# FFN's first products in another order, operands' sums product by product, and the final norm's last squares summed by TensorE

## The chip, the cores and the metric

The kernel runs on one core of one Trainium2 chip. The metric is the device time of one execution in microseconds (us), the median over several runs. Line numbers are those of the kernel before; the profile gives one execution, instruction by instruction.

## The reference

One layer on a sequence of 1024 rows with 1024 channels, float32. What matters here comes after the two mixers:

```python
mix = jnp.einsum('bsd,de->bse', g_a * y_a + g_b * y_b, w_o[l])
x = x + g1 * mix
h2 = rms_norm(x, norm_ffn_g[l]) * (1.0 + sc2) + sh2
a, bgate = jnp.split(jnp.einsum('bsd,df->bsf', h2, w_ffn_in[l]), 2, axis=-1)     # 1024 -> 2 x 2816
x = x + g2 * jnp.einsum('bsf,fd->bsd', jax.nn.silu(a) * bgate, w_ffn_out[l])
return rms_norm(x, final_norm_g)
```

## The kernel before, in words

**Layout and precision.** Activations lie with channels on the 128 partitions and the sequence along the free axis, in two halves of 512 columns (KC = 8 blocks of 128 channels, KH = 4 is half of them). Each float32 operand is split in a high part, rounded by ScalarE (`wh`, `t2h` and so on, a cast), and a low part, the difference, made by VectorE (`wl`, `t2l`). A product of two such operands is three matmuls (`mm3`, lines 289, 290 and 292: high by high, high by low, low by high).

**Duals.** The FFN's input matrix is worked off in N_IN = 11 duals. A dual is two column blocks of weights by two halves of the sequence, computed with seven products in place of eight, in the order `PRODUCTS = "1265734"`. Each product is 24 matmuls of 128x512: two banks p of 4 blocks k of 3. Operands of the products: 1 and 2 take parts of h2 as they are (`h20` to `h27`, the first half of the sequence); 6 takes `t2`; 5 takes `t1`; 7 takes `t3`; 3 takes `b22`; 4 takes `t4`. These are sums and differences of h2's quarters; they are the same for every dual and are made once, at the start of the FFN. Products 1, 6, 7 and 4 accumulate one after the other in the banks x, products 5 and 3 in the banks z, product 2 in y; ahead of each next product that accumulates there, the bank must have been read (`in_evac`: copies by ScalarE for 1, 6 and 5, additions by VectorE for 2, 7 and 3).

**Weights.** `load` issues a 512 KB DMA on SP's queue into one of five buffers `raw` (`raw_tile`); a later load waits until a buffer is free. `split_w` casts (line 208) and subtracts (line 209). `next_w` keeps two units of the list `plan` ahead of the product that runs. In `dual_units` the blocks 11 and 12 are the weights of products 1 and 2; 6, 5, 7 and 3 need sums of blocks (lines 231, 232, 233 and 235). A dual with `early` loads its blocks one by one as units need them, and block 11 twice; otherwise product 1's unit loads all four.

**The start of the FFN.** The order before is: products 1 and 2 of dual 0, then of dual 1; then dual 0's other five; then dual 1's; then duals 2 to 10, seven each. While the first four run, the second half's norm is finished: `mix` evicts the output projection (line 813) and sums the squares (line 821), an `ss` matmul adds over partitions (line 410), and `rstd_end` (lines 344 to 346) makes two Newton-type steps on ScalarE's approximate reciprocal root. `norm_2_half(k)` then makes one fourth of t2; `norm_2_last` makes all operands for products 5, 7, 3 and 4. `tc.issue_after(ins)` puts what it encloses behind `ins` in its engine's list; apart from such rules the order on each engine comes from the framework's scheduler.

**The end.** The output product's last part runs in `PIECES` of 512, 256 and 256 columns. `piece_out` does one block j of 8: 12 matmuls, an eviction on VectorE (line 1078), a square on ScalarE (line 1081) and, for blocks scaled on GpSimd, a multiplication by the final gain (line 1085). `piece_sum` adds the squares on VectorE (line 1090). The norm of a piece is begun after block NORM_AT = 2 of the next one and its scaling after block NORM_AT + 3; the last piece's follow its last block. `piece_scale` multiplies by the reciprocal root: pieces 0 and 1 on GpSimd, in the last piece blocks 0, 3 and 5 on GpSimd (line 1101) and five on VectorE (line 1103), and issues the output DMAs.

Of the kernel before, what the change touches and what calls it, by code (L numbers as in the profile page):

```python
# [39 lines left out]
P = 128  # L40
D = 1024
T = 1024
# [48 lines left out]
NORM_AT = 2  # L91
LAG = 2
POOL_LAST = (0, 3, 5)
# [13 lines left out]
FILL = 272  # L107
# [3 lines left out]
def block_kernel(ctx: ExitStack, tc: tile.TileContext, x0, xT, c, vecs, ada, w_first, w_plain, w_duals,  # L111
# [102 lines left out]
    def dual_units(mats, n, early=False, eng=nc.vector):  # L214
# [7 lines left out]
        def unit(m):  # L222
            if early:
                get(*{"1": ("11",), "2": ("12",), "6": ("21", "22", "11"), "3": ("12",), "4": ("22",)}.get(m, ()))
            elif m == "1":
                get("11", "12", "21", "22")
            if m in "12":
                return split_w(a["1" + m], n, (), eng)
            if m == "6":
                a["s1"] = a["22"] if early else raw_tile(n)  # L230
# [70 lines left out]
    def product(banks, m, t, evac=None, between=None, y_tile=ps2_tile):  # L301
# [4 lines left out]
        for p in range(2):  # L306
            if m in "125":
                banks[b, p] = (y_tile if b == "y" else ps_tile)(b)
# [18 lines left out]
    def t_split(src, hi, lo):  # L327
        nc.scalar.copy(hi, src)  # L328
        t_split.ins = nc.vector.tensor_tensor(lo, src, f32(hi), ALU.subtract).ins  # L329
# [528 lines left out]
    def norm_2_last():  # L858


        def splits(m, name, srcs):
            for k, src in enumerate(srcs):
                ts[m][k] = t_pair(name)
                t_split(src, *ts[m][k])
# [3 lines left out]
        with tc.issue_after(t_split.ins):  # L868
            splits("5", "t1", [x1[k][:, halves[0]] for k in range(KH)])
            for k in range(KH):  # L870
                nc.vector.tensor_tensor(b12[k], b22[k], b12[k], ALU.subtract)
        with tc.issue_after(t_split.ins):
            splits("7", "t3", b12)
        with tc.issue_after(t_split.ins):
            splits("3", "b22", b22)
        with tc.issue_after(t_split.ins):
            for k in range(KH):
                minus(b21[k], t2[k], b21[k])
            splits("4", "t4", b21)
# [12 lines left out]
    in_units = [dual_units([w_fi[d, m] for m in range(4)], 1024, d < 2) for d in range(N_IN)]  # L892
    in_order = [(d, m) for d in range(2) for m in "12"] + [(d, m) for d in range(2) for m in PRODUCTS[2:]]
    in_order += [(d, m) for d in range(2, N_IN) for m in PRODUCTS]

    def in_unit(d, m):
        if (d, m) == (1, "6"):
            with tc.issue_after(t_split.ins):
# [12 lines left out]

    def in_evac(d):
        def evac(p, m, ps):
# [6 lines left out]
            elif m == "7":  # L920
                t = ha[f, "5"]
                nc.vector.tensor_tensor(t, ps, t, ALU.add)
                nc.scalar.activation(t, t, AF.Silu, scale=-1.0)
            elif m == "3":
                t = ha[f, "6"]
                nc.vector.tensor_tensor(t, ps, t, ALU.add)
# [49 lines left out]
    def in_product(d, m):  # L976
        product(in_banks[d], m, ts[m], in_evac(d), y_tile=ps_tile if d == 1 else ps2_tile)
        if d == N_IN - 1:
            group_load(0, m)

    def norm_2_start():
        nonlocal r2
        r2 = norm_start(sums[1], "r2")

    r2 = None
    product(in_banks[0], "1", ts["1"], in_evac(0), norm_2_start)
    r2 = rstd_end(*r2)
    for i, (d, m) in enumerate(in_order[1:4]):
        norm_2_half(i, r2)
        in_product(d, m)  # L990
    norm_2_half(KH - 1, r2)
    norm_2_last()
    close(*phase_1)
    raws.append(open_pool("raw_a", 1, side="right", stack=ctx)[1])
    x1ap = open_pool("x1a", 2, side="right", stack=ctx)[1]
    phase_2 = [open_pool("gi", 7), open_pool("stage", 3, side="right")]
    gip, stagep = (p for _, p in phase_2)
    for d, m in in_order[4:]:
# [4 lines left out]
        if m == PRODUCTS[-1]:  # L1003
            if 2 <= d < 6:
                with tc.issue_after(in_evac.ins):
                    for i in range(40 + 2 * (d - 2), 42 + 2 * (d - 2)):
                        modulation(i, x1ap.tile([P, T], F32, tag="x1", name="ada"))
# [61 lines left out]
    def piece_out(i, j):  # L1069
# [14 lines left out]
        if on_pool(i, j):  # L1084
            nc.scalar.activation(dst, dst, AF.Copy, scale=col(V_GFIN, j))
# [113 lines left out]
```

## Time and profile before

| what | value |
|---|---|
| median of 3 runs | 1516.14 us (1514.99 to 1517.78) |
| the profiled execution's own time | 1518.37 us |
| its span in the profile | 1516.6 us |
| mean granted TensorE clock | 0.992 |
| busy: TensorE, VectorE, ScalarE, GpSimd | 1480.1, 1177.6, 612.7, 582.0 us |
| the FFN's first product starts | near 853.7 us |
| the last matmul of the output product | 1501.54 us |

Times in the views count from the span's start. PE is TensorE, DVE VectorE, ACT ScalarE, POOL GpSimd, SP the queue that issues loads. A row of a timeline holds start, duration, engine, line, operation, output<-inputs, and in brackets the idle time before it with its releaser. A row of the waits holds who waited for whom, the total in us, the number of times and the longest. "x2" merges two instructions.

### The profile page before, as it was taken

How to read it: one execution, taken by the hardware profiler on the slowest of the kernel's cores; microseconds unless marked ns; L12 is line 12 of the kernel's file. 1: busy time of each engine (PE TensorE's matmuls, PEld its weight loads, DVE VectorE, ACT ScalarE, POOL GpSimd, SP SyncE). 2: the span in 40 equal slices, each digit the busy share in tenths (PEclk: the TensorE clock that was granted, in tenths of full speed). 3: DMA queues.
4: the chain of work that ended last, by engine and by line, in shares of the span. 5: the costliest groups of instructions: out<-in, count | busy, mean ns of one | idle time of the engine just before them, and what ended most of it. 6: DMA issues, size and time to landing. Idle time of an engine off the chain costs nothing.

```text
span 1516.6 us, 17958 instructions
## 1 busy us (share of the span) xinstructions
PE 1480.1 (98%) x6529; PEld 1211.6 (80%) x6529; DVE 1177.6 (78%) x1566; ACT 612.7 (40%) x871; POOL 582.0 (38%) x483
## 2 busy tenths in 40 slices
PE   9999999999998999999999989999999999999996
PEld 5788887877886888888788868888888888888886
DVE  7897898999998881858877798777777665676756
ACT  4654333433332442335335464444444443212234
POOL 0037788788768884320121001000111016535005
PEclk9999999999999999999999999999999999999998
DMA  9512223223222159647765436455554449999303
GB/s 345 207 63 84 84 70 139 70 97 111 98 83 87 66 198 393 242 152 223 251 207 163 143 97 193 156 179 179 181 172 158 155 152 365 354 292 282 124 15 112
DMA packets 87307, 255.66 MB, mean 169 GB/s; under 512 B 10033, under 2 KB 12209, under 8 KB 87218
## 3 DMA queue, kind: packets, MB, share of 16 engines
q1 hardware_dynamic: 46384, 146.30, 28.9%
q0 software_dynamic: 36944, 95.44, 19.1%
q10 hardware_dynamic: 3890, 12.78, 2.1%
q8 instruction: 51, 0.84, 0.2%
q14 instruction: 38, 0.31, 0.1%
HBM read 187.89 MB, written 66.58 MB: 168 GB/s over the span
## 4 chain that ended last, share of the span: by engine, by line
PE 50%; DVE 1%; ACT 1%; issue 0%; DVEq 0%; ACTq 0%
PE x L289 7%; PE x L290 7%; PE x L292 7%; PE z L289 4%; PE z L290 4%; PE z L292 4%; PE y L290 3%; PE y L289 3%; PE y L292 3%; PE mix L289 2%; PE mix L290 2%; PE mix L292 2%; PE yb L289 1%; PE yb L290 1%; PE yb L292 1%
## 5 line engine op out<-in xcount | busy, mean ns | idle before, releaser
L208 ACT CAST wh<-raw 128x1024 fp32r<-128x1024 f32 (+2 forms) x257 | 259.1, 1009 | 422.9 <-PE x L290 107.3
L209 POOL TENSOR_TENSOR wl<-raw,wh 128x1024 fp32r<-128x1024 f32 x92 | 238.0, 2594 | 86.5 <-ACT wh L208 80.1
L209 DVE TENSOR_TENSOR wl<-raw,wh 128x1024 fp32r<-128x1024 f32 (+2 forms) x165 | 188.2, 1141 | 52.4 <-ACT wh L208 50.2
L663 DVE SCALAR_TENSOR_TENSOR c<-diff,vec,c 128x512 f32<-128x512 f32 x248 | 182.3, 749 | 6.4 <-DMA q<-qs 2.6
L942 POOL DMA_DIRECT2D hid<-stage x71 | 37.9, 534 | 356.5 <-DVE stage L329 351.0
L289 PE MATMUL x<-th,wh 128*128 128x512 f32 x336 | 130.8, 389 | 0.0
L292 PE MATMUL x<-th,wl 128*128 128x512 f32 x336 | 130.7, 389 | 0.0
L290 PE MATMUL x<-tl,wh 128*128 128x512 f32 x336 | 130.7, 389 | 0.0
L663 DVE SCALAR_TENSOR_TENSOR c<-u,wsum,c 128x512 f32<-128x512 f32 x112 | 84.0, 750 | 7.1 <-issue 5.1
L292 PE MATMUL x<-t2h,wl 128*128 128x512 f32 x184 | 72.9, 396 | 4.2 <-POOL wl L209 4.2
L289 PE MATMUL x<-t2h,wh 128*128 128x512 f32 x184 | 72.2, 394 | 2.8 <-ACT t2h L328 2.4
L289 PEld LDWEIGHTS x<-th,wh 128*128 128x128 f32 x336 | 63.1, 188 | 13.3 <-issue 0.2
L290 PEld LDWEIGHTS x<-tl,wh 128*128 128x128 f32 x336 | 63.1, 188 | 13.1
L292 PEld LDWEIGHTS x<-th,wl 128*128 128x128 f32 x336 | 63.1, 188 | 13.1
L290 PE MATMUL x<-t2l,wh 128*128 128x512 f32 x184 | 72.5, 394 | 0.0
L231 POOL TENSOR_TENSOR raw<-raw 128x1024 f32<-128x1024 f32 x12 | 29.3, 2439 | 99.5 <-DVE wl L209 95.7
L292 PE MATMUL z<-th,wl 128*128 128x512 f32 x168 | 65.5, 390 | 0.0
L289 PE MATMUL z<-th,wh 128*128 128x512 f32 x168 | 65.4, 389 | 0.0
L290 PE MATMUL z<-tl,wh 128*128 128x512 f32 x168 | 65.4, 389 | 0.0
L328 ACT CAST stage<-g 128x512 fp32r<-128x512 f32 x62 | 38.3, 621 | 56.4 <-DMA hid<-stage 33.4
L270 DVE CUSTOM_DVE_ANT_0 raw<-raw,cs,vec 128x1024 f32<-128x1024 f32 x24 | 34.1, 1424 | 32.3 <-DMA raw<-in_ada 20.0
L329 DVE TENSOR_TENSOR stage<-g,stage 128x512 fp32r<-128x512 f32 x62 | 42.3, 687 | 21.7 <-ACT stage L328 21.6
(799 smaller groups left out, 4095.3 us busy)
## 6 DMA issues: line engine op xcount, KB each, us to landing
hid<-stage POOLq DMA_DIRECT2D x71, 512.0 KB, 4.8
raw<-in_w_fi SPq DMA_DIRECT2D x50, 512.0 KB, 4.2
raw<-in_w_duals SPq DMA_DIRECT2D x48, 512.0 KB, 3.5
th<-hid POOLq DMA_DIRECT2D x71, 256.0 KB, 6.1
tl<-hid POOLq DMA_DIRECT2D x71, 256.0 KB, 6.2
ada<-in_ada SPq DMA_DIRECT2D x24, 512.0 KB, 6.0
raw<-in_ada SPq DMA_DIRECT2D x24, 512.0 KB, 4.7
raw<-in_w_fo SPq DMA_DIRECT2D x24, 384.0 KB, 6.0
```

The source lines that it names most:

```text
L208: nc.scalar.copy(wh, raw)
L209: lo = lo_engine.tensor_tensor(wl, raw, f32(wh), ALU.subtract)
L231: eng.tensor_tensor(a["s1"], a["21"], a["22"], ALU.add)
L270: nc.vector.tensor_tensor_reduce(out=raw, in0=raw, in1=cs, scale=1.0, scalar=col(V_ADA, b), op0=ALU.mult, op1=ALU.add, accum_out=modc(b),)
L289: nc.tensor.matmul(ps, wh, xh, start=first, stop=False, skip_group_check=again)
L290: nc.tensor.matmul(ps, wh, xl, start=False, stop=False, skip_group_check=again)
L292: mm3.ins = nc.tensor.matmul(ps, wl, xh, start=False, stop=last, skip_group_check=again).ins
L328: nc.scalar.copy(hi, src)
L329: t_split.ins = nc.vector.tensor_tensor(lo, src, f32(hi), ALU.subtract).ins
L663: tap.ins = nc.vector.scalar_tensor_tensor(out=out, in0=src[:, s : s + H], scalar=wt, in1=acc, op0=ALU.mult, op1=ALU.add).ins
L942: nc.gpsimd.dma_start(hid_dram[key], s)
```

## The change

Five things are changed together.

- **Order.** Dual 2's product 1 runs after dual 1's product 2, ahead of dual 0's product 6. Dual 2's blocks are loaded in two steps (11 alone for product 1; 12, 21, 22 and 11 again for product 2), and its banks x are copied only ahead of its product 2. The banks y of dual 1 and z of duals 0 and 2 come from the pool of two banks (`ps2`).
- **Sums product by product.** `norm_2_last` is replaced by `norm_2_sums(m)`, called for m = 5, 7, 3 and 4 ahead of dual 0's product m; each is put behind the splits of the one before on VectorE and ScalarE. So are the weight units of dual 0's products 7, 3 and 4, and dual 0's additions to the banks of 7 and 3 (`behind_sums`, VectorE alone).
- **Final norm's steps.** The Newton step is written in two VectorE instructions with a square on ScalarE (`piece_norm`, `piece_rstd`); the sign that this changes is taken back by a negated gain `ngf`. The intermediate lies in PSUM, in the last piece the result too, with a copy in SBUF for GpSimd (`rp`).
- **Last squares.** In the last piece the squares of the last three blocks are not added by VectorE; `ss` is summed by TensorE from four operands.
- **Places.** NORM_AT is 1 instead of 2, the scaling follows two blocks later instead of three, and an unused fill tile has 264 columns instead of 272.

The diff, cut to its core:

```diff
-NORM_AT = 2
+NORM_AT = 1
 LAG = 2
+APART = 3
...
-FILL = 272
+FILL = 264
...
         def unit(m):
-            if early:
+            if early == 2:
                 get(*{"1": ("11",), "2": ("12",), "6": ("21", "22", "11"), "3": ("12",), "4": ("22",)}.get(m, ()))
+            elif early:
+                get(*{"1": ("11",), "2": ("12", "21", "22", "11")}.get(m, ()))
...
     def t_split(src, hi, lo):
-        nc.scalar.copy(hi, src)
+        t_split.act = nc.scalar.copy(hi, src).ins
...
-    def norm_2_last():
...
-        with tc.issue_after(t_split.ins):
-            splits("5", "t1", [x1[k][:, halves[0]] for k in range(KH)])
+    def norm_2_sums(m):
...
+        with tc.issue_after(t_split.ins), tc.issue_after(t_split.act):
             for k in range(KH):
-                nc.vector.tensor_tensor(b12[k], b22[k], b12[k], ALU.subtract)
...
+                if m == "7":
+                    nc.vector.tensor_tensor(b12[k], b22[k], b12[k], ALU.subtract)
+                elif m == "4":
+                    minus(b21[k], t2[k], b21[k])
             for k in range(KH):
-                minus(b21[k], t2[k], b21[k])
-            splits("4", "t4", b21)
+                ts[m][k] = t_pair("t" + m)
+                t_split({"5": x1[k][:, halves[0]], "7": b12[k], "3": b22[k], "4": b21[k]}[m], *ts[m][k])
...
-    in_units = [dual_units([w_fi[d, m] for m in range(4)], 1024, d < 2) for d in range(N_IN)]
-    in_order = [(d, m) for d in range(2) for m in "12"] + [(d, m) for d in range(2) for m in PRODUCTS[2:]]
-    in_order += [(d, m) for d in range(2, N_IN) for m in PRODUCTS]
+    EARLY = [2, 2, 1] + [0] * (N_IN - 3)
+    in_units = [dual_units([w_fi[d, m] for m in range(4)], 1024, EARLY[d]) for d in range(N_IN)]
+    in_order = [(0, "1"), (0, "2"), (1, "1"), (1, "2"), (2, "1")] + [(d, m) for d in range(2) for m in PRODUCTS[2:]]
+    in_order += [(d, m) for d in range(2, N_IN) for m in PRODUCTS if (d, m) != (2, "1")]
...
     def in_unit(d, m):
-        if (d, m) == (1, "6"):
-            with tc.issue_after(t_split.ins):
+        if (d, m) in ((0, "7"), (0, "3"), (0, "4"), (1, "6")):
+            with tc.issue_after(t_split.ins), tc.issue_after(t_split.act):
...
-    def in_product(d, m):
-        product(in_banks[d], m, ts[m], in_evac(d), y_tile=ps_tile if d == 1 else ps2_tile)
+    def in_product(d, m, between=None):
+        late = EARLY[d] == 1
+        if late and m == "2":
+            for p in range(2):
+                in_evac(d)(p, "1", in_banks[d]["x", p])
+        product(in_banks[d], m, ts[m], None if late and m == "1" else in_evac(d), between,
+                z_tile=ps2_tile if d in (0, 2) else ps_tile)
...
-    norm_2_half(KH - 1, r2)
-    norm_2_last()
...
+    for i, (d, m) in enumerate(in_order[5:]):
+        if i < 4:
+            norm_2_sums("5734"[i])
...
     def piece_scale(i, rf):
         at, n = PIECES[i]
         m = H // n
+        if i == LAST:
+            rp = wide_tile("rp")[:, :n]
+            nc.scalar.copy(rp, rf)
+        else:
+            rp = rf
...
-                    nc.gpsimd.tensor_tensor(y, src, rf, ALU.mult)
+                    nc.gpsimd.tensor_tensor(y, src, rp, ALU.mult)
...
-    def piece_norm(i, acc):
-        return norm_start(acc, "rf", PIECES[i][1], wide_tile)
+    def piece_norm(i, parts):
+
+        n = PIECES[i][1]
+        ss, r, q = (t[:, :n] for t in (ps_tile("ss"), wide_tile("rf"), wide_tile("rq")))
+        for part in parts:
+            nc.tensor.matmul(ss, ones, part, start=part is parts[0], stop=part is parts[-1])
+        rstd_start(ss, eps1, "rf", n, lambda name: r)
+        nc.scalar.activation(q, r, AF.Square, scale=0.5 ** 0.5)
+        return ss, r, q
+
+    def piece_rstd(i, ss, r, q):
+
+        n = PIECES[i][1]
+        t = ps2_tile("rft")[:, :n]
+        nc.vector.scalar_tensor_tensor(out=t, in0=ss, scalar=EPS, in1=q, op0=ALU.add, op1=ALU.mult)
+        out = ps2_tile("rf")[:, :n] if i == LAST else r
+        nc.vector.scalar_tensor_tensor(out=out, in0=t, scalar=1.5, in1=r, op0=ALU.subtract, op1=ALU.mult)
+        return out
...
-            if j > lag:
+            if j > lag and j - lag < KC - APART * (i == LAST):
                 piece_sum(i, j - lag)
...
-                norm = piece_norm(i - 1, acc)
-            if i and j == NORM_AT + 3:
+                norm = piece_norm(i - 1, [acc])
+            if i and j == NORM_AT + 2:
...
-        for j in range(KC - lag, KC):
-            piece_sum(i, j)
-    piece_scale(LAST, rstd_end(*piece_norm(LAST, sqs[0])))
+    piece_scale(LAST, piece_rstd(LAST, *piece_norm(LAST, [sqs[0]] + sqs[KC - APART :])))
```

58 lines of the change are left out of this document (28 added, 30 removed).

## The prediction

> **What bounds the kernel now.** I read the page's busy table first, then TensorE's waits over the whole run.
>
> ```profile
> span 1516.6 us, 17958 instructions
> PE 1480.1 (98%) x6529; PEld 1211.6 (80%) x6529; DVE 1177.6 (78%) x1566; ACT 612.7 (40%) x871; POOL 582.0 (38%) x483
> ...
> PE ss L410 <- DVE sq L1090: 3.9, 1, 3.9
> PE z L289 <- ACT g L917: 3.7, 1, 3.7
> PE x L289 <- ACT t2h L328: 2.4, 1, 2.4
> ...
> PE lead L289 <- ACT h11h L364: 1.4, 1, 1.4
> ```
>
> TensorE is busy 98% of the span, so only its holes can be won. The change touches the three rows that open the wait list: two where the FFN's first products begin (z, x) and one in the last norm (ss). After the last matmul nothing hides VectorE, so there every instruction on the path counts.
>
> The first place by the table of windows (us; then TensorE, its weight loads, VectorE, ScalarE, GpSimd busy; granted clock; DMA):
>
> ```profile
> 870.91:876.35 5.44, 5.44 (x25) 4.50 (x24) 5.44 (x9) 3.27 (x5) 0.00 (x0) 1.00 0.33 96
> 876.35:908.78 32.43, 26.30 (x97) 19.82 (x96) 29.05 (x43) 19.90 (x31) 0.00 (x0) 0.89 0.31 98
> 884.73:888.14 3.41, 3.41 (x9) 2.65 (x8) 3.41 (x7) 3.26 (x6) 0.00 (x0) 0.50 0.00 0
> 901.79:905.20 3.41, 3.41 (x9) 2.64 (x10) 3.38 (x6) 2.77 (x4) 0.00 (x0) 0.50 0.86 303
> 860.79:907.68 46.89, 40.76 (x162) 31.78 (x161) 43.46 (x64) 27.83 (x44) 0.00 (x0) 0.93 0.29 90
> ```
>
> Row one is an undisturbed product, dual 1's product 2: 24 matmuls in 5.44 us. Row two is dual 0's products 6, 5, 7 and 3: 96 matmuls, 21.8 us at that pace, which took 32.43. So 10.7 us are lost: 6.1 idle (2.4 and 3.7), 3.4 in the two half-clock stretches of rows three and four (1.7 each), 1.2 in small waits. The last row is VectorE from the second norm's first Newton step to the end of dual 1's sums: 43.5 of 46.9 us busy. VectorE feeds all of this, so any work put on it there comes out later.
>
> **Part 1: dual 2's product 1 goes ahead of dual 0's product 6.** It adds 5.44 us of matmuls as cover, and takes them out of the steady part later, where TensorE is the bound. It also adds one 512 KB load (dual 2's 11 block comes twice), and all later loads move back one place in SP's queue. That queue is paced by VectorE, since a load starts when a weight split has freed its buffer:
>
> ```profile
> 848.69 1.22 DVE L231 TENSOR_TENSOR raw<-raw 128x1024 f32<-128x1024 f32 x1 [3.13 <-DMA raw<-in_w_fi]
> 850.50 1.21 DVE L209 TENSOR_TENSOR wl<-raw,wh 128x1024 fp32r<-128x1024 f32 x1
> 853.75 0.75 DVE L813 SCALAR_TENSOR_TENSOR x<-mix,mod,xr 128x512 f32<-128x512 f32 x1 [1.44 <-PE mix L292]
> 854.65 1.23 DVE L209 TENSOR_TENSOR wl<-raw,wh 128x1024 fp32r<-128x1024 f32 x1
> 860.79 0.69 DVE L344 SCALAR_TENSOR_TENSOR r2t<-r2r 128x512 f32<-128x512 f32 x1
> 844.99 0.33 SPq L194 DMA_DIRECT2D raw<-in_w_fi  x1
> 851.74 0.33 SPq L194 DMA_DIRECT2D raw<-in_w_fi  x1
> 848.13 1.05 ACT L208 CAST wh<-raw 128x1024 fp32r<-128x1024 f32 x1 [3.84 <-PE mix L290]
> ```
>
> The load of 844.99 landed when L231, the first sum, started: 3.7 us. The split of 850.50 ended at 851.71 and the next load left at 851.74. In the changed kernel's lists the first sum needs the load after that split. Without a sum ahead of it the split starts when its cast ends (849.2) and ends at 850.4; the load lands at 854.1 and the sum ends at 855.3. Queued behind it on VectorE is the last mix eviction, which starts then instead of at 853.75. The next split ends at 857.2 instead of 855.9, its load lands at 860.9, the second and third sums (1.2 each) follow, and the Newton step starts at 863.2 instead of 860.79: 2.4 us later. TensorE itself loses about 0.4 us on the way, waiting for the squares' sum. The new unit's cast falls into ScalarE's idle time (27.8 of 46.9 us busy); its bank is copied only ahead of dual 2's product 2; dual 1's product 2 now takes the banks of dual 0's and must wait for their two evictions, which, four VectorE steps behind the start of the Newton step, end near 867.5; TensorE comes to it at 871.
>
> Is the first hole covered? The last t2 cast now:
>
> ```profile
> 882.57 0.62 ACT L328 CAST t2h<-t 128x512 fp32r<-128x512 f32 x1 [1.82 <-DVE t L333]
> ```
>
> It ends at 883.2; 2.4 later, less a VectorE wait of some 0.5 that falls away, is 885.1. TensorE comes to product 6 at 876.35 + 0.4 + 5.44 = 882.2 and has 12 matmuls (2.7 us) ahead of that operand: 884.9. Covered, to a few tenths.
>
> **Part 2: sums and splits product by product.** The 3.7 us hole was no missing operand: product 3 waited for ScalarE to copy product 5's bank, and ScalarE had four t4 casts and an idle time ahead of the copies. In the new ScalarE list those copies stand ahead of product 3's casts, and VectorE's order is product 5's splits, 7's, 3's, 4's, as TensorE needs them. Walking the lists with the rows' durations, I find each operand of 5, 7, 3 and 4 ready before its matmul.
>
> What is late next is dual 1's product 6. Its three sums still stand behind all of dual 0's splits on VectorE. The cover that hid them was the hole.
>
> ```profile
> 906.46 1.22 DVE L233 TENSOR_TENSOR raw<-raw 128x1024 f32<-128x1024 f32 x1
> 907.77 2.10 ACT L208 CAST wh<-raw 128x1024 fp32r<-128x1024 f32 x2 [3.08 <-DVE raw L233]
> 908.20 1.22 DVE L235 TENSOR_TENSOR raw<-raw 128x1024 f32<-128x1024 f32 x1
> 909.34 1.22 DVE L209 TENSOR_TENSOR wl<-raw,wh 128x1024 fp32r<-128x1024 f32 x1
> 911.07 0.68 DVE L926 TENSOR_TENSOR g<-z,g 128x512 f32<-128x512 f32 x1
> ```
>
> VectorE's work from the Newton step to the third sum's end was 43.5 us; now it also holds one weight split (1.2), the sum for dual 0's product 3 (1.2), formerly ahead of the Newton step, and two evictions that have moved ahead (0.7 each): 47.3. From 863.2, with some 0.4 of idle, that is 910.9, and the cast (1.05) ends at 912. TensorE finishes product 4 at 876.35 + 0.4 + 6 x 5.44 = 909.4. So a new hole of about 2.5 us, and some 0.5 more for the split behind it: 3.0.
>
> Does it cost a half-clock stretch too? Holes of 2.4 and 3.7 us did, the one of 1.4 shows none after it. I take it: 1.7. [...]
>
> Part 1 and 2 together: 10.7 - 0.4 - 3.0 - 1.7 = 5.6 us won.
>
> **Part 3: the last norm.**
>
> ```profile
> 1501.54 0.28 PE L292 MATMUL y<-th,lwl 128*128 128x256 f32 x1
> 1505.76 1.07 PE L410 MATMUL ss<-sq,ones 128*128 128x256 f32 x2 [3.94 <-DVE sq L1090]
> 1494.20 0.43 PE ss L410 x2
> 1500.02 1.51 DVE L344 SCALAR_TENSOR_TENSOR rft<-rfr 128x256 f32<-128x256 f32 x1
> 1501.57 0.48 DVE L345 SCALAR_TENSOR_TENSOR rft<-ss,eps,rft 128x256 f32<-128x256 f32 x1
> 1503.03 0.48 DVE L1078 SCALAR_TENSOR_TENSOR x<-y,mod,x 128x256 f32<-128x256 f32 x1
> 1503.54 0.42 ACT L1081 ACTIVATE sq<-x 128x256 f32<-128x256 f32 x1 [0.65 <-DVE x L1078]
> 1506.87 0.47 ACT L339 ACTIVATE rfr<-ss,eps 128x256 f32<-128x256 f32 x1 [2.82 <-PE ss L410]
> 1509.52 3.47 DVE L1103 SCALAR_TENSOR_TENSOR y<-x,vec,rfr 128x256 f32<-128x256 f32 x5
> 1490.40 10.84 POOL L1101 TENSOR_TENSOR x<-x,rfr 128x512 f32<-128x512 f32 x8 [85.74 <-DVE rfr L346]
> 1502.94 6.26 POOL L1101 TENSOR_TENSOR y<-x,rfr 128x256 f32<-128x256 f32 x8 [1.70 <-ACT sq L1081]
> 1509.65 2.66 POOL L1101 TENSOR_TENSOR y<-x,rfr 128x256 f32<-128x256 f32 x3 [0.45 <-DVE rfr L346]
> ```
>
> Now: the last matmul ends at 1501.8, its eviction starts at 1503.03 because VectorE works on piece 1's Newton steps, three sums follow, TensorE sums at half clock from 1505.76, and VectorE scales until 1512.99; 3.6 us later the span ends. Two VectorE steps, L344 (1.51) and the five scalings (0.69 each), run beside GpSimd with both inputs in SBUF; steps with one input in PSUM take 0.48 beside it (the row of 1503.03).
>
> After, in this time frame: the norm of piece 1 comes one piece and its scaling two pieces earlier, so VectorE is free and evicts at once, until 1502.3; the square ends at 1502.8. TensorE adds up four operands (0.43 each at full clock, as at 1494.20, for it hardly idles): the first three follow the last matmul, the fourth ends at 1503.6. ScalarE's reciprocal root (0.47) and the new square (0.42): 1504.6. Two VectorE steps with PSUM operands (0.48 each; the trace has no step that also writes PSUM at this width, bounds 0.4 and 0.7): 1505.7. ScalarE's copy for GpSimd (0.4): 1506.2. Its three multiplications (0.89 each, and it is free by then: its piece 1 ended at 1509.2 and moves forward by at least two blocks of 12 matmuls of half the width of row one, 2.8 us, to 1506.4): 1508.8; VectorE's five are done by 1508.1. Two output DMAs are issued after GpSimd's last, so 0.3 more, and 3.6 to the end: 1512.7. Won: 3.9 us, bounds 2.5 (PSUM steps at 0.7, GpSimd late by 1) and 5.
>
> [...]
>
> At nothing: the negated gains, one small VectorE step that waits for vec at the start, ahead of the first squares' sum; that sum feeds an ss matmul behind the clock matmuls. The fill's 8 columns do no work. **Sum:** 5.6 + 3.9 = 9.5 us.
>
> **Rivals.** (a) The new hole at dual 1's product 6 stays short or at full clock, if VectorE is 1 to 2 us ahead of my walk: 1.7 to 4.7 us more, 1502 to 1505. Against it: VectorE has no idle time left there. (b) The loads land later. Two of them stand in series ahead of the Newton step, so each us of landing costs 2. Seen in this stretch:
>
> ```profile
> DMA to landing us min/median/max: 3.5/3.6/5.0
> ```
>
> At 5.0 the gain is 9.5 - 2.6 = 6.9: 1509.2. (c) The other side, by the same mechanism: from 3.7 + 9.5 / 2 = 8.5 us of landing on, the change is slower; at 10 us it takes 1519.2. For it: GpSimd's stores and loads share the DMA engines. Against it: nothing here came near. (d) The reordering does not do what it says: product 3 still waits 3.7 us and its half clock 1.7, so only 4.1 are won: 1512. Against it: the copies' place in the list.
>
> **How the numbers follow.** The profiled execution took 1518.37 us for its 1516.6 span, 2.2 above the median of the runs, 1516.14. On it the sum gives 1508.9; on the median 1506.6, which is the forecast. Chances: forecast 0.52, (a) 0.2, (b) 0.13, (d) 0.05, (c) 0.06, gain lost to small things within 0.2% (3 us, about what a measurement of this kernel can tell from no change) 0.04. Faster 0.9, same 0.04, slower 0.06. The range reaches into (a) and over (b): 1502 to 1511.
>
> **What would show it.** Right: TensorE's waits list no t2h and no z wait; a wait of 2 to 3 us for dual 1's first cast near 909 with a 0.50 stretch behind it; the second norm's Newton step near 863; the four sums without a half clock and the end some 11 us after the last matmul instead of 14.8. Wrong: a t2h wait over 1 us, a wait elsewhere in the FFN, an unchanged tail.

## The result, and the profile after

The changed kernel takes 1506.55 us (median of 6 runs, 1503.49 to 1509.06) beside 1516.83 for the kernel before (6 runs, 1514.99 to 1518.97): a ratio of 0.9932, 95% interval 0.9918 to 0.9946, or 10.3 us less, 8.2 to 12.4. The forecast was 9.5 less, counted from the first three runs of the kernel before (median 1516.14).

From here on the lines are those of the changed kernel. Its profiled execution took 1503.49 us, the fastest of the six. First the page's span and busy times, as shown of before:

```profile
span 1501.7 us, 17958 instructions
PE 1477.5 (98%) x6535; PEld 1210.7 (81%) x6535; DVE 1170.8 (78%) x1561; ACT 613.3 (41%) x875; POOL 580.6 (39%) x483
```

Then TensorE's waits in the same profile (who waited for whom, total us, times, longest):

```profile
PE x L297 <- POOL wl L211: 6.1, 5, 3.0
...
PE x L294 <- ACT wh L210: 2.1, 1, 2.1
...
PE ss L415 <- DVE xr L826: 0.3, 1, 0.3
```

The three rows that the prediction set out to remove (ss 3.9, z 3.7, t2h 2.4) are gone. The prediction says that they open before's list. They do not: GpSimd's splits, in the unchanged mixers ahead of the FFN, led it then as now, with this row of before:

```profile
PE x L292 <- POOL wl L209: 7.4, 4, 2.9
```

In place of the three stands one wait of 2.1 us for the cast of dual 1's weights for product 6. The wait of 0.3 for the second norm's sum of squares is the small loss that the prediction put at 0.4.

Two things have to be separated before the spans are compared. The FFN's first matmul and the output product's last one cut the run in three. The two rows are from the changed kernel's timeline:

```profile
850.51 0.39 PE L294 MATMUL x<-h20h,wh 128*128 128x512 f32 x1
...
1491.25 0.28 PE L297 MATMUL y<-th,lwl 128*128 128x256 f32 x1
```

The FFN starts at 850.51, against 853.55 in before's profile: 3.0 us of the 14.9 between the two spans lie ahead of anything that was changed. From the FFN's first matmul to the end of the last one pass 1491.53 - 850.51 = 641.0 us (before: 1501.82 - 853.55 = 648.3), and 1501.7 - 1491.5 = 10.2 us from there to the end (before 14.8). So the FFN's start won 7.2 us in this pair of profiles and the final norm 4.6. The lead ahead of the FFN came out between 850.1 and 854.9 us in the profiles of this study, with the same code there but for one small VectorE step (the negated gains); so below every kernel is read by these two stretches, not by its span.

| kernel | median, us | ratio to before (95%) | FFN to last matmul, us | last matmul to end, us |
|---|---|---|---|---|
| before | 1516.83 | | 648.3 | 14.8 |
| changed | 1506.55 | 0.9932 (0.9918 to 0.9946) | 641.0 | 10.2 |
| changed, second time | 1505.79 | 0.9927 (0.9914 to 0.9941) | 641.7 | 10.2 |
| changed, third time | 1507.5 | 0.9941 (0.9929 to 0.9953) | 642.8 | 10.2 |
| FFN's half alone | 1509.34 | 0.996 (0.9948 to 0.9972) | 642.7 | 14.7 |
| final norm's half alone | 1512.59 | 0.9976 (0.9967 to 0.9984) | 649.6 | 10.5 |
| without the early product | 1507.25 | 0.9942 (0.993 to 0.9954) | 644.7 | 10.3 |
| without the new lists | 1509.19 | 0.9955 (0.9942 to 0.9968) | 644.3 | 10.5 |
| all squares added by VectorE | 1507.61 | 0.9943 (0.9929 to 0.9957) | 642.6 | 12.1 |
| root in SBUF | 1507.2 | 0.9938 (0.9924 to 0.9951) | 642.4 | 10.3 |
| norm's steps late | 1507.4 | 0.9934 (0.9919 to 0.9949) | 642.5 | 11.4 |
| second cover | 1506.84 | 0.9929 (0.9917 to 0.9941) | 639.5 | 10.9 |
| second cover, again | 1504.22 | 0.9916 (0.9903 to 0.993) | 639.4 | 10.9 |

Each ratio stands against runs of the kernel before that were made beside it. Their medians were 1516.83 for the first row of the changed kernel; 1515.85 for the two halves, the kernel without the early product and the one without the new lists; 1516.59 for the second time of the changed kernel, all squares added by VectorE, root in SBUF and the second cover's first run; 1516.29 for the other three.

How VectorE came to dual 1's sums, in the changed kernel's timeline:

```profile
857.79 1.23 DVE L237 TENSOR_TENSOR raw<-raw 128x1024 f32<-128x1024 f32 x1 [3.02 <-DMA raw<-in_w_fi]
860.20 0.68 DVE L349 SCALAR_TENSOR_TENSOR r2t<-r2r 128x512 f32<-128x512 f32 x1
...
906.45 1.22 DVE L238 TENSOR_TENSOR raw<-raw 128x1024 f32<-128x1024 f32 x1
```

The Newton step stands at 860.20, which is 863.24 once the 3.04 of the earlier start are added back; the forecast was 863.2. The wait of 3.02 for a load ahead of it is what delayed it. The third sum of dual 1 ends at 907.67, or 910.7; the forecast was 910.9. TensorE's side of it, in the same profile:

```profile
906.32 0.39 PE L297 MATMUL x<-t4h,wl 128*128 128x512 f32 x1
908.80 0.50 PE L294 MATMUL x<-t2h,wh 128*128 128x512 f32 x1 [2.10 <-ACT wh L210]
```

ScalarE's copies of product 5's banks, for which product 3 had waited 3.7 us, now stand ahead of product 3's casts:

```profile
889.33 0.58 ACT L917 COPY g<-z 128x512 f32<-128x512 f32 x1
890.42 0.59 ACT L917 COPY g<-z 128x512 f32<-128x512 f32 x1 [0.51 <-PE z L297]
890.90 1.14 ACT L333 CAST t3h<-x 128x512 fp32r<-128x512 f32 x2
```

And the end of the run, TensorE, VectorE, ScalarE and GpSimd in turn:

```profile
1491.37 1.89 PE L1131 MATMUL ss<-sq,ones 128*128 128x256 f32 x8
1491.57 0.48 DVE L1091 SCALAR_TENSOR_TENSOR x<-y,mod,x 128x256 f32<-128x256 f32 x1 [0.49 <-PE y L297]
1494.25 0.43 DVE L1140 SCALAR_TENSOR_TENSOR rft<-ss,rq 128x256 f32<-128x256 f32 x1 [2.19 <-ACT rq L1133]
1494.72 0.43 DVE L1142 SCALAR_TENSOR_TENSOR rf<-rft,rf 128x256 f32<-128x256 f32 x1
1495.59 2.05 DVE L1121 SCALAR_TENSOR_TENSOR y<-x,ngf,rf 128x256 f32<-128x256 f32 x5 [0.44 <-ACT rp L1110]
1493.30 0.47 ACT L344 ACTIVATE rf<-ss,eps 128x256 f32<-128x256 f32 x1 [0.70 <-PE ss L1131]
1495.19 0.37 ACT L1110 COPY rp<-rf 128x256 f32<-128x256 f32 x1 [0.97 <-DVE rf L1142]
1495.64 2.09 POOL L1119 TENSOR_TENSOR y<-x,rp 128x256 f32<-128x256 f32 x3 [1.23 <-ACT rp L1110]
```

The last eviction starts 0.04 us after its matmuls are done (the last one ends at 1491.53), the four sums end at 1493.26, VectorE's five scalings take 2.05 where they took 3.47, and GpSimd's three 2.09 where they took 2.66.

### The profile page after: what moved, and what is told of

Its sections match the earlier page's. It is cut to its first block, busy times and chain, and to the rows that moved or that the text cites. A ratio compares the mean times of both kernels' runs of the same rounds, so it can differ in the third digit from the quotient of the medians.

```text
span 1501.7 us, 17958 instructions
## 1 busy us (share of the span) xinstructions
PE 1477.5 (98%) x6535; PEld 1210.7 (81%) x6535; DVE 1170.8 (78%) x1561; ACT 613.3 (41%) x875; POOL 580.6 (39%) x483
## 4 chain that ended last, share of the span: by engine, by line
PE 48%; DVE 2%; issue 0%; POOL 0%; ACT 0%; POOLq 0%; DMA 0%; DVEq 0%; ACTq 0%
PE x L297 7%; PE x L295 7%; PE x L294 7%; PE z L295 4%; PE z L297 4%; PE z L294 4%; PE y L295 3%; PE y L297 3%; PE y L294 3%; PE mix L295 2%; PE mix L294 2%; PE mix L297 2%; PE yb L294 1%; PE yb L295 1%; PE yb L297 1%; DVE wl L211 1%
```

## The experiments

### Each half alone, and the FFN's two edits one at a time

**FFN's half alone.** The changed kernel with before's final norm:

```diff
-NORM_AT = 1
+NORM_AT = 2
...
-    piece_scale(LAST, piece_rstd(LAST, *piece_norm(LAST, [sqs[0]] + sqs[KC - APART :])))
+    piece_scale(LAST, rstd_end(*piece_norm(LAST, sqs[0])))
```

> The FFN's half of the change alone: the new order and the sums product by product as in the changed kernel, the final norm as before. Theory: the two halves do not touch each other, so this wins what the prediction's Parts 1 and 2 hold. With the hole at dual 1's product 6 at 2.1 us and no half-clock stretch behind it that is 10.7 - 0.4 - 2.1 - 0.3 = 7.9 at most, with a stretch behind it 1.7 less: 6.2 to 7.9 us, 1508.6 to 1510.3 on a median of 1516.5. The trace should show the hole once more: a wait of 2 to 2.5 us for dual 1's cast, and no wait for t2h or z. Rival: the FFN's gain was mostly luck of the profiled run (3.0 us of the difference of the two traces lie ahead of the change) and the final norm carries the result: then under 4 us, 1512.5 or more.

Measured: 0.996, or 6.1 us less (4.2 to 7.9). TensorE's waits in it show the same hole and neither z nor t2h:

```profile
PE x L294 <- ACT wh L210: 2.1, 1, 2.1
```

The table of windows for the hole and the 3.4 us behind it (us; busy TensorE, its loads, VectorE, ScalarE, GpSimd; granted clock; DMA):

```profile
909.50:912.90 3.40, 1.64 (x6) 1.06 (x7) 3.40 (x5) 3.07 (x5) 0.00 (x0) 1.00 0.00 0
912.90:916.30 3.40, 3.40 (x10) 2.62 (x9) 3.40 (x5) 2.26 (x4) 0.54 (x1) 0.50 0.25 67
```

Here the hole is followed by half clock, in the changed kernel's first profile it was not. The theory holds, and at the lower end of its span (6.2 to 7.9), as it should with the stretch there. The rival (under 4 us) lies outside the interval.

**Final norm's half alone.** The kernel before with the changed kernel's lines from `piece_out` on, `ngf`, NORM_AT = 1 and APART = 3:

```diff
-    piece_scale(LAST, rstd_end(*piece_norm(LAST, sqs[0])))
+    piece_scale(LAST, piece_rstd(LAST, *piece_norm(LAST, [sqs[0]] + sqs[KC - APART :])))
```

> The final norm's half alone: the FFN's start as before, the norm's two-step Newton with PSUM operands, the last three squares added up by TensorE, norm and scaling of a piece earlier. Theory: 4.6 us, as the two traces have it between the last matmul and the end (14.8 before, 10.2 after): 1511.9 on a median of 1516.5. The trace should show 10.2 us behind the last matmul, and t2h 2.4 and z 3.7 among TensorE's waits as before. Rival: TensorE's extra sums and the changed order cost the output product something ahead of the last matmul, so that less than 3 us are left: 1513.5 or more.

Measured: 0.9976, 3.6 us less (2.4 to 5.0), with 10.5 us behind the last matmul. Its waits keep both old holes:

```profile
PE z L290 <- ACT g L918: 3.7, 1, 3.7
...
PE x L290 <- ACT t2h L329: 2.4, 1, 2.4
```

The expected 4.6 is inside the interval, and so is the rival's 3. The last stretch favours the theory (4.3 less than before), but the stretch ahead of the last matmul is 1.3 us longer than in before's profile, which is what the rival says. Its cause there is not the extra sums. Behind the z hole this profile has two windows of half clock, where before's had one (us; busy TensorE, its loads, VectorE, ScalarE, GpSimd; granted clock; DMA):

```profile
898.23:901.64 3.41, 2.70 (x6) 2.15 (x7) 3.41 (x7) 3.28 (x6) 0.00 (x0) 0.50 0.60 185
901.64:905.05 3.41, 3.41 (x9) 2.64 (x8) 3.34 (x4) 0.38 (x1) 0.00 (x0) 0.50 0.30 123
```

Product 3, which runs there, took 3.0 us over the 5.44 of an undisturbed product, against 1.7 in before's profile. So what the kernel before loses behind the same hole differs by chance, too. 6.1 and 3.6 are 9.7, the whole change 10.3: within the intervals the halves add up.

**Without the early product.** Dual 2's product 1 back among its own:

```diff
-    EARLY = [2, 2, 1] + [0] * (N_IN - 3)
+    EARLY = [2, 2] + [0] * (N_IN - 2)
...
-    in_order = [(0, "1"), (0, "2"), (1, "1"), (1, "2"), (2, "1")] + ...
+    in_order = [(0, "1"), (0, "2"), (1, "1"), (1, "2")] + ...
```

> The changed kernel without dual 2's product 1 ahead of dual 0's product 6 (dual 2 as in the kernel before, banks y and z as before); sums product by product and the new final norm stay. Theory: each half of the FFN's edit fills a hole of its own. Without the cover the wait for t2h comes back, 2.4 to 3 us, with its half-clock stretch of 1.7 behind it; the wait for z stays away; VectorE has one weight split less and starts 2.4 us earlier, so dual 1's third sum ends near 907 instead of 910.7 in the frame of the kernel before and the hole at dual 1's product 6 shrinks to 0 to 2 us. Together 2 to 4 us slower than the changed kernel: 1508.5 to 1510.5. Rival: what counts is VectorE's work up to dual 1's sums, and the early product only moves the hole: then within 1 us of the changed kernel, 1505.5 to 1507.5.

Measured: 0.9942, which is 0.2 to 2.3 us slower than the changed kernel by the three ratios of that one (0.9927, 0.9932, 0.9941); the intervals overlap, and the median, 1507.25, lies in the rival's range and not in the theory's. Its FFN took 644.7 us, 1.9 to 3.6 more than the changed kernel's and 2.1 more than the mean of the five profiles that, like this one, have half clock behind the hole at dual 1's product 6 (642.6). TensorE's waits:

```profile
PE x L294 <- ACT wh L210: 2.2, 1, 2.2
...
PE x L294 <- ACT t2h L333: 1.2, 1, 1.2
```

The theory is half right. The t2h wait comes back, but at half the size and without a half clock. The third sum ends at 906.2, which is 54.0 us behind the FFN's first matmul at 852.2; in the changed kernel it is 907.7 - 850.5 = 57.2. So the sums did come 3.2 us earlier, but TensorE came earlier by as much (its hole begins 52.9 us behind its start instead of 56.2), and the hole at dual 1's product 6 did not shrink. That is the rival's picture: both holes hang on one chain of VectorE's work. VectorE also lost part of its earlier start at once, waiting for a cast, a wait that the changed kernel does not have (its Newton step and the split behind it, at 860.20 and 860.80, follow each other):

```profile
857.46 0.68 DVE L349 SCALAR_TENSOR_TENSOR r2t<-r2r 128x512 f32<-128x512 f32 x1
860.02 1.23 DVE L211 TENSOR_TENSOR wl<-raw,wh 128x1024 fp32r<-128x1024 f32 x1 [1.88 <-ACT wh L210]
```

**Without the new lists.** `norm_2_last` as before, called ahead of dual 0's product 6; no places of their own for dual 0's weight units and additions:

```diff
-        if (d, m) in ((0, "7"), (0, "3"), (0, "4"), (1, "6")):
-            with tc.issue_after(t_split.ins), tc.issue_after(t_split.act):
+        if (d, m) == (1, "6"):
+            with tc.issue_after(t_split.ins):
...
-        if i < 4:
-            norm_2_sums("5734"[i])
+        if i == 0:
+            norm_2_last()
```

> The changed kernel with the kernel before's order of the sums and splits (all made at one go ahead of dual 0's product 6, weight units of dual 0 and its additions without a place of their own); dual 2's product 1 stays early, the new final norm stays. Theory: no wait for t2h, since the cover stays; the wait for z comes back, since ScalarE's copies of product 5's banks stand behind the t4 casts again, 3.7 us or more, as the casts come out some 3.6 us later and TensorE only some 1.7 us later: 4 to 6 us, with 1.7 of half clock behind it; the hole at dual 1's product 6 (2.1) goes. Together 3 to 6 us slower than the changed kernel: 1509.5 to 1512.5. Rival: with 5.4 us more of TensorE's work in front the copies come in time, and the order of the lists is worth nothing: within 1 us of the changed kernel.

Measured: 0.9955, 2.1 to 4.2 us slower than the changed kernel by its three ratios, FFN 644.3 us. The one large wait of the FFN's start:

```profile
PE z L294 <- ACT g L926: 3.7, 1, 3.7
```

And the place of the copies that it waits for, on ScalarE:

```profile
897.88 2.42 ACT L333 CAST t4h<-x 128x512 fp32r<-128x512 f32 x4 [2.38 <-DVE x L338]
900.21 1.06 ACT L926 COPY g<-z 128x512 f32<-128x512 f32 x2
```

The wait for z is back, with a half-clock stretch behind it, and the copies stand behind the four t4 casts again; the wait for the weights' cast and the one for t2h are not there. This is the theory's picture, a little below its sizes (it had a hole of 4 to 6 us and 1509.5 or more; 3.7 and 1509.19 were measured), and it names the lists as the cause of the z hole: the early product alone did not bring ScalarE's copies in time. In the FFN's stretch the early product alone wins 4.0 (648.3 to 644.3), the lists alone 3.6 (648.3 to 644.7), and both together 5.5 to 7.3, less than the sum, for together they leave the hole at dual 1's product 6.

### The final norm's steps

The medians of these three kernels (1507.2 to 1507.61) do not part them from the changed kernel (1505.79 to 1507.5). They are read by the last stretch, from the last matmul to the end, which was 10.17 to 10.23 us in the changed kernel's three profiles.

**All squares added by VectorE:**

```diff
-APART = 3
+APART = 0
...
+    for j in range(KC - LAG, KC):
+        piece_sum(LAST, j)
     piece_scale(LAST, piece_rstd(LAST, *piece_norm(LAST, [sqs[0]] + sqs[KC - APART :])))
```

> The changed kernel with all squares of the last piece added on VectorE again (the last two behind the last eviction), so that TensorE sums one operand. Theory: between the last square and the sum over partitions stands one VectorE addition more, 0.4 us and a handover, and TensorE, idle for about 2 us by then, may do its one sum at half clock, 0.4 more: 0.6 to 1.1 us slower than the changed kernel; the trace should show 10.8 to 11.3 us from the last matmul of the output product to the end instead of 10.2. Rival: the fourth sum of TensorE waits for the last square just as VectorE's addition would, and the whole gain of the final norm comes from VectorE being free and the PSUM operands: then within 0.3 us.

Measured: 12.1 us behind the last matmul, 1.9 more than the changed kernel. The timeline:

```profile
1495.50 0.70 PE L1131 MATMUL ss<-sq,ones 128*128 128x256 f32 x2 [2.89 <-DVE sq L1103]
1493.05 2.40 DVE L1103 TENSOR_TENSOR sq<-sq 128x256 f32<-128x256 f32 x3
1492.72 3.31 POOL L1119 TENSOR_TENSOR y<-x,rf 128x256 f32<-128x256 f32 x4
```

The rival falls. The theory's direction holds, its size was too small: three additions, not one, are left when the last eviction is done, and each takes 0.80 beside GpSimd instead of the 0.4 expected (before's at 1502.69, done for the most part ahead of GpSimd's, took 0.42). Undone alone, the squares that TensorE adds cost 1.9 of the final norm's 4.6 us.

**Root in SBUF:**

```diff
         if i == LAST:
-            rp = wide_tile("rp")[:, :n]
-            nc.scalar.copy(rp, rf)
+            rp = rf
...
-        out = ps2_tile("rf")[:, :n] if i == LAST else r
+        out = r
```

> The changed kernel with the last piece's root written to SBUF instead of PSUM, read from there by VectorE and GpSimd alike; ScalarE's copy for GpSimd falls away. Theory: VectorE with both inputs in SBUF and GpSimd hinder each other: VectorE's five scalings take 0.69 each as in the kernel before (3.47) and GpSimd's three 0.89 (2.66); both start 0.4 us earlier, so VectorE ends at 0.4 + 2.05 from the second Newton step's end instead, 1.0 us later than in the changed kernel, and the end comes 0.7 to 1.3 us later. Rival: where the operand lies is of no account, the five scalings stay near 2.05 us and the end comes 0.4 us earlier.

Measured: 10.3 us behind the last matmul, as in the changed kernel. Its timeline, with the output DMAs' issues:

```profile
1499.59 3.47 DVE L1120 SCALAR_TENSOR_TENSOR y<-x,ngf,rf 128x256 f32<-128x256 f32 x5
1499.73 2.66 POOL L1118 TENSOR_TENSOR y<-x,rf 128x256 f32<-128x256 f32 x3 [0.90 <-DVE rf L1141]
1502.41 0.37 SPq L1123 DMA_DIRECT2D outT<-y  x1
1503.09 0.37 SPq L1123 DMA_DIRECT2D outT<-y  x1
```

The engines did exactly what the theory says: 3.47 and 2.66, the figures of the kernel before. But the end hardly moved. The changed kernel's last two issues:

```profile
1497.76 0.37 SPq L1124 DMA_DIRECT2D outT<-y  x1
1498.23 0.45 SPq L1124 DMA_DIRECT2D outT<-y  x1
```

There VectorE's last output, done at 1497.64, stands in SP's queue behind one that waits for GpSimd (done at 1497.73). It is issued 0.47 behind that one, and the end comes 3.5 us later (1501.7). With the root in SBUF the last issue is 0.45 later counted from the last matmul (1503.09 - 1495.94 = 7.15 against 1498.23 - 1491.53 = 6.70), but the end comes 3.1 us after it. So the PSUM operand won VectorE 1.4 us, and the end moved by less than 0.1: theory and rival both missed. Why the last output took 0.4 less here is open. That it is issued 0.68 behind its neighbour does not explain it: in the FFN's half alone it is issued 0.67 behind, and the end came 3.5 after it.

**Norm's steps late:**

```diff
-NORM_AT = 1
+NORM_AT = 2
...
-            if i and j == NORM_AT + 2:
+            if i and j == NORM_AT + 3:
```

> The changed kernel with a piece's norm begun after block 2 and its scaling after block 5 of the next piece, as in the kernel before. Theory: VectorE's two steps for piece 1 and GpSimd's eight multiplications (6.1 us in the changed kernel, done 1.2 us before GpSimd's next work) move two blocks of 1.2 to 1.4 us later, so GpSimd comes to its last three multiplications 1.2 to 1.6 us late, and the end is 12 us behind the last matmul instead of 10.2. Rival: only VectorE's freedom at the last eviction counts, and it has 0.5 us of idle time there: then the end stays within 0.4 us of 10.2.

Measured: 11.4 us behind the last matmul, 1.2 more: less than the theory's 1.8 and more than the rival's 0.4. In its timeline

```profile
1496.87 1.99 PE L1131 MATMUL ss<-sq,ones 128*128 128x256 f32 x8 [0.69 <-DVE sq L1103]
1496.74 0.47 DVE L1091 SCALAR_TENSOR_TENSOR x<-y,mod,x 128x256 f32<-128x256 f32 x1
1498.90 0.47 ACT L344 ACTIVATE rf<-ss,eps 128x256 f32<-128x256 f32 x1 [1.15 <-PE ss L1131]
1501.47 2.09 POOL L1119 TENSOR_TENSOR y<-x,rp 128x256 f32<-128x256 f32 x3
```

the last eviction starts 0.57 behind the last matmul (1496.17) instead of 0.04, TensorE waits 0.69 for VectorE's sum, and ScalarE's root starts 2.73 behind the last matmul instead of 1.77: 1.0 us of VectorE's work. GpSimd, which the theory blamed, is only 0.2 late for its last three (0.68 behind the start of ScalarE's copy at 1500.79, against 0.45 in the changed kernel). So the cause is the rival's, VectorE at the last eviction, but its idle time of 0.5 did not take up the work.

Undone one at a time, the three steps cost 1.9, less than 0.1 and 1.2 us of the 4.6. The Newton step in two VectorE instructions was not undone by itself, so what it wins of the rest is not shown.

### The hole that is left

**The changed kernel, a second and a third time**, for the clock behind the hole:

> The changed kernel unaltered, beside the next three on one chip, and a second profile of its new hole. The hole of 2.1 us at dual 1's product 6 had no half-clock stretch behind it in the first profile and had one in the profile of the FFN's half alone. Theory: the granted clock is set by windows of 3.41 us on a grid that starts anew with each run; a window that is idle for about 1.9 us or more is followed by half clock, one with 1.7 or less is not, so a hole of 2.1 us is followed by one in about half of the runs, by where it falls. Then this profile's hole follows that rule whichever it is: half clock if one window holds 1.9 us of it, none if the grid cuts it. Rival: the length alone decides (2.1 us never, 2.4 always) and the stretch in the other profile came from a second wait: then none here.

> The changed kernel unaltered once more, as the other half of the comparison with the next kernel, and one more profile of the hole at dual 1's product 6. Theory of the grid: half clock behind the hole if one window of 3.41 us holds 1.9 us or more of it, none if it holds 1.5 or less, either between; the FFN's stretch from its first product to the last matmul then takes 642.4 to 642.7 us with the half clock and 641 to 641.7 without. Rival: the stretch varies by more than the half clock explains.

In each profile the half-clock stretches start on one grid of 3.413 us, which gives its windows (in before's at 464.89, 481.95, 884.72 and 901.79, or 5, 118 and 5 steps apart). Those of the second profile of the changed kernel at the hole:

```profile
907.45:910.86 3.41, 2.39 (x11) 1.65 (x9) 3.41 (x5) 1.17 (x3) 0.00 (x0) 1.00 0.32 130
910.86:914.27 3.41, 2.29 (x9) 1.59 (x10) 3.41 (x5) 3.41 (x5) 0.00 (x0) 1.00 0.00 0
```

and the kernel with the root in SBUF, whose FFN is the same:

```profile
908.60:912.01 3.41, 1.34 (x7) 0.80 (x5) 3.41 (x6) 1.76 (x3) 0.00 (x0) 1.00 0.01 2
912.01:915.42 3.41, 3.41 (x8) 2.72 (x9) 3.41 (x6) 2.79 (x4) 0.00 (x0) 0.50 0.00 0
```

The hole is 2.1 us long in both. In the first the grid cuts it (1.0 and 1.1 us idle), and the clock stays; in the second one window has all of it (2.07 idle), and the next is at half. Of the seven profiles with this hole five have the stretch and two have none.

TensorE's idle time in all windows of that grid was counted from the trace in the thirteen profiles of this study, from 15 us on to TensorE's last instruction. Of the windows at full clock with more than 0.9 us idle, those with 1.93 or more were followed by half clock 33 times of 33, those with 1.65 or less by full clock 55 times of 55, and of the seven between (1.66 to 1.86) two by half. A window already at half clock was followed by another one at half when it was itself idle for 0.67 to 0.86 us (3 of 3), and by full clock with 0.55 or less (32 of 32); that is how the z hole of the final norm's half came to cost two. The rival, that the length decides, falls. With the stretch the FFN takes 642.4 to 642.8 us, without it 641.0 and 641.7.

What the hole and the stretch cost can be read by products, since an undisturbed one takes 5.44 us. In the third profile of the changed kernel, dual 0's products 6 and 4 and dual 1's product 6 take

```profile
881.39:887.44 6.05, 5.79 (x25) 4.35 (x24) 5.10 (x8) 4.24 (x8) 0.00 (x0) 1.00 0.30 87
903.77:911.43 7.66, 5.60 (x25) 4.32 (x23) 7.66 (x12) 2.47 (x5) 0.00 (x0) 1.00 0.40 137
911.43:918.75 7.32, 7.32 (x24) 5.59 (x25) 7.32 (x10) 4.54 (x7) 1.07 (x2) 0.77 0.42 107
```

The first row lost 0.6 us (a wait of 0.3 for t2h is in it), the second, which ends with the hole, 2.2, and the third, with the stretch, 1.9. Over the five profiles with the stretch the third loses 1.9 in the mean; in the two without it, 0.5. So the stretch costs 1.4 us.

**A second cover.** Dual 2's product 2 between dual 0's product 4 and dual 1's product 6, dual 2's blocks loaded one by one:

```diff
-    EARLY = [2, 2, 1] + [0] * (N_IN - 3)
+    EARLY = [2, 2, 3] + [0] * (N_IN - 3)
...
-    in_order = [...] + [(d, m) for d in range(2) for m in PRODUCTS[2:]]
+    in_order = [...] + [(0, m) for m in PRODUCTS[2:]]
+    in_order += [(2, "2")] + [(1, m) for m in PRODUCTS[2:]]
...
-            if early == 2:
+            if early >= 2:
```

> A version that could beat both kernels: dual 2's product 2 is put between dual 0's product 4 and dual 1's product 6 as well, its 5.44 us of matmuls as cover for dual 1's three sums; dual 2's blocks are loaded one by one like those of duals 0 and 1 (two 512 KB loads more), the rest is the changed kernel. Theory: VectorE has a weight split (1.2) and two steps that wait for product 4 ahead of the third sum, TensorE comes 5.44 us later, so the hole of 2.1 us goes and with it the half-clock stretch of 1.7 that stands behind it in some runs: 2 to 3.8 us faster than the changed kernel run beside it. Rival: the two more loads and VectorE's split make a hole of the same size elsewhere, at dual 2's product 2 or at dual 1's products: within 1 us of the changed kernel.

> The version with dual 2's product 2 as a second cover, unaltered. In its first run its FFN took 639.45 us from the first product to the last matmul, against 641.0 to 642.7 for the changed kernel's FFN, yet its median was not lower than that of the changed kernel beside it (1506.84 and 1505.79), because its profiled run had reached the FFN 1.9 us later. Theory: the lead into the FFN is chance (850.1 to 854.9 us in runs with the same code ahead of it), so it wins 1.6 to 3.2 us over many runs: 1503 to 1505 here beside 1506 for the changed kernel, with an FFN of 639 to 640 us in the profile. Rival: something in it delays the way to the FFN or the end by as much, so that its FFN starts after 854 again and the medians agree within 1 us.

Its windows where the hole was:

```profile
906.00:916.00 10.00, 10.00 (x44) 8.00 (x44) 10.00 (x14) 3.48 (x8) 0.00 (x0) 1.00 0.43 157
```

TensorE is busy throughout at full clock. The FFN took 639.5 and 639.4 us, 1.6 to 3.4 less than the changed kernel's. In the first run the median was no lower, in the second 3.3 us lower. The mean of its nine runs is 1505.14, that of the ten of the changed kernel beside it 1506.85: 1.7 us less. The rival of the first run (another hole of that size) falls by the profile. The second's is partly right: its FFN started at 854.9 in one run and 851.7 in the other, so its later start in the first run was not the cover's doing, but in both the end lies 10.9 us behind the last matmul instead of 10.2, with the engines' last work in the same places. The last output is issued 0.1 later, and from there to the end pass 4.1 and 4.0 us instead of 3.5; why is open. It is the fastest of all kernels here: in the second comparison all four of its runs (1502.67 to 1504.78) lie under all five of the changed kernel's (1506.48 to 1509.07), in the first they mix.

## Why the prediction was right

The forecast, 1506.6, is 0.05 us from the median. That closeness is luck: the other two medians of the same kernel are 1505.79 and 1507.5, and in the difference to before, 9.5 was forecast and 10.3 measured. The mechanisms were right, with misses that partly cancel. By its own steps:

- **Bound and holes.** The three holes named are the ones that went, though they did not open the wait list. The 1.2 us that the step puts down to small waits are not waits: in that window the list has the holes of 3.7 and 2.4 and no others, and the rest is in matmuls, most of them next to the holes, that start 0.26 to 0.39 us apart instead of 0.23. Each experiment that undid an edit brought its own hole back: without the lists z at 3.7, without the early product t2h (at 1.2, not 2.4).
- **Part 1.** The Newton step at 863.24 against 863.2 and the ss wait of 0.3 against 0.4 show the delay by one load in series as it was worked out. Rivals (b) and (c), later loads, did not occur: the loads of this stretch landed 3.5 to 3.7 us after their issue. The cover of t2h was close, as the step said ("to a few tenths"): in the seven profiles there was no wait four times and 0.2 to 0.7 three times. The sum had nothing for it, but dual 0's product 6 took 0.5 us over its 5.44 in the mean of the five profiles with the stretch.
- **Part 2.** The z wait went for the reason given, the copies' place in ScalarE's list, and rival (d) is out. The sum had 3.0 for the new hole and the split behind it; 2.2 and 0.5 were lost there in the profiles without the stretch, so it had 0.3 too much.
- **The half clock behind it.** 1.7 was taken. That term has no one value: it stood in five of seven profiles, at 1.4 us. The first profile, which lacks it, looked like rival (a), for another reason than (a) gives: VectorE was not ahead of the walk (910.7 against 910.9), the grid cut the hole. With the stretch the FFN's start wins 648.3 - 642.6 = 5.7, close to the 5.6 of the sum, but only because 0.6 too much for hole and stretch stands against the 0.5 at dual 0's product 6. And before's side rests on one profile: the same FFN start took 1.3 us more in the profile of the final norm's half. In the profiles half clock went with the idle time in one window of the grid: 1.93 of its 3.41 us or more were followed by it in all 33 cases, while the hole of 2.1 us was followed by it five times of seven. So the step's reason, that a hole's length decides, failed, though its value was the likelier one.
- **Part 3.** 3.9 was predicted; the last stretch shrank by 4.6 in the profile, and the half alone won 3.6 by the runs (2.4 to 5.0). Mis-sized were GpSimd's three multiplications, 0.70 each for 0.89 (0.6 us of the chain), and the two VectorE steps, 0.43 for 0.48. VectorE also waited 0.44 for ScalarE's copy, which the step had not seen; it cost nothing, as GpSimd was done later still. The kernel before makes one Newton step in three VectorE instructions (lines 344 to 346), not two steps; the changed kernel makes that step in two. That GpSimd gains too when VectorE reads PSUM, the root in SBUF shows: 2.66 against 2.09 for GpSimd and 3.47 against 2.05 for VectorE. In before's profile, with the same 3.47 and 2.66, both engines started one instruction each about every 0.87 us, in turns (VectorE at 1509.92, 1510.79 and 1511.65, GpSimd at 1509.65, 1510.55 and 1511.41). What no step had: a difference of 0.45 us in the last output's issue moved the end by less than 0.1.

## What to carry to other kernels

When TensorE waits, ask first on whose list the releasing instruction stands behind other work: here the lists' order, with a copy moved ahead of four casts, was worth by itself about as much (3.6 us) as 5.4 us of cover (4.0), and both together 5.5 to 7.3. A cover ahead of a chain that one engine is working off only moves the hole unless the cover is longer than what the chain still holds, so look for the next operand on the same engine. Compare kernels by stretches between named instructions; a lead with unchanged code differed by up to 4.9 us between profiles, half of what the change was worth.

## What the hardware showed

- The TensorE clock followed windows of 3.41 us on a grid that lay elsewhere against the program from profile to profile (its last line ahead of the FFN's first matmul came 2.96 us before it in the kernel before, 0.13 in the changed one's first profile). A window at full clock that was idle for 1.93 us or more cost half clock in the next (33 of 33), one with 1.65 or less did not (55 of 55); a window at half clock kept the next at half when it was idle for 0.67 us or more (3 of 3), and not with 0.55 or less (32 of 32). The hole of 2.1 us was therefore followed by half clock, at a cost of 1.4 us, in five profiles of seven and not in the other two, and behind a hole of 3.7 us the next product lost 1.7 in one profile and 3.0 in another.
- VectorE's 128x256 additions with both inputs in SBUF took 0.80 us each beside GpSimd, and its scalings 0.69; with one input in PSUM the scalings took 0.41 and GpSimd's multiplications fell from 0.89 to 0.70.
- From the last output DMA's issue to the end passed 3.47 to 3.59 us in ten of the thirteen profiles, whether it was issued 0.48, 0.67 or 0.79 behind the one before it. In the kernel with the root in SBUF it was 3.1, with the second cover 4.0 and 4.1, and why is open.
